# Two-layer mixer with split fp32 products: high weights times both activation halves in one matmul

## The chip, the cores and the metric

The kernel runs on one core of a Trainium2 chip. The metric is the device time of one execution in microseconds (us). The kernel before takes 1300.45 us (median of three runs, 1300.34 to 1304.79).

## The reference

One decoder layer on 256 tokens of 1024 features, all in float32. What matters here is the first half, the token mixer:

```
h = RMSNorm(x) * (1 + scale1) + shift1
z = h @ W_in       # 1024 x 9216: u v p xc B C and the gates gA gB gC, 1024 columns each
A  = W_A( u * (tril(W_s) v + b) )
Bp = scale * GroupLinear( trailing_mean_w(p) - p ),  w in 2,4,8,16
Cv = W_C( B * causal_dwconv3( C * xc ) )
x = x + gate1 * W_o( sig(gA)*A + sig(gB)*Bp + sig(gC)*Cv )
```

Then a router picks 4 of 32 experts for each token; their weights (32 x 12 MB in float32) are read from HBM one expert pair after the other, and a last RMSNorm follows.

## The kernel before

TensorE does the mixer's products in a one-pass format (fp32r). To keep float32 accuracy each operand is split in two parts, a rounded high part and the remainder (low part), and a product is the sum of three: high weights times high activations, high weights times low activations, low weights times high activations. The activations are kept as pairs: a tile `[P, 2, KB, T]` has in its second index the high (0) and the low part (1); `hp` is the pair of h, `apair` that of the branches' inner results, `fin["p"]` that of the gated sum. The weights are split as they are used: `split` (L503 to L509) has ScalarE (ACT) write the high part of 512 columns (L507) and VectorE (DVE) subtract it to get the low part (L508), into one of four buffers named `spl`.

The work is a list of steps. A `col_item` makes 128 output features of one of the products for all 256 tokens. It consists of two half-steps, each with one split of 4 x 128 weight columns and one call of `pair3` (L511): four times the two matmuls with the high weights (L515, L516), then four with the low weights (L518), all 128x256 and all accumulating into the same 256 columns of one PSUM bank (`abank`, six banks in turn). `u_item` is one such half-step with its own bank, `pool_item` has two output blocks of six matmuls for one split. When the last half-step of an item is through, an evacuation function reads the bank:

- `u_item`'s evac: first half a copy on ACT (L626), second half an addition on DVE (L628)
- `sig_evac` for gA, gB, gC: a sigmoid on ACT (L827)
- `pa_evac`, `c_evac`, `b_evac`, `pc_evac`: a product on DVE (L832, L883, L890, L898)
- `p_evac`, `xc_evac`: a copy on ACT (L838, L879); `pool_item`'s evac: a scaled product on DVE (L869)

`to_pair` (L435, L436) then splits a finished result for the next product, high part on ACT, low part on DVE. The steps `v` and `wo` do not use `pair3`; they issue their own matmuls of 512 or 256 columns (L556 to L560, L976).

The order on every engine is written out by the loop at L1036 (`AHEAD = 3`): before step i's matmuls are issued, the splits of the steps ahead are issued (at most four live), then step i's matmuls, then a row or so of the adaLN product (`weigh_rows`, L443 on DVE, `spread` there), then what is due, then the evacuation of step i-1. ACT and DVE work in the order of issue. The items come in this order: u, gA, pA, p and gB by turns, pool with xc, C, B, xc, C, B, gC, pC, wo.

Loads run through SyncE's queue into a ring of seven 2 MB slots (`lay`, `issue`, L176); a slot is loaded again when the work that read it has been issued and is done. The ring feeds the mixer and, behind it, the experts.

## Time and profile before

| | |
|---|---|
| median of three runs | 1300.45 us |
| the profiled execution | 1302.01 us, its span 1300.3 us |
| mean granted TensorE clock | 0.984 |
| PE busy | 1211.8 us (93%) |
| DVE busy | 439.8 us (34%) |
| ACT busy | 270.8 us (21%) |
| HBM read | 482 MB, 372 GB/s over the span |

The profile shows one execution. PE is TensorE's matmuls, PEld its weight loads, DVE VectorE, ACT ScalarE. An instruction has a start and a duration; neighbouring ones on one engine overlap by their durations, so the distance of two starts is what one more of them takes. The mixer lasts until about 336 us, the router follows, and the experts take the rest.

### The profile page before, as it was taken

To read this page: it belongs to the slowest core of one execution; us is meant where nothing else is said; L and a number is where in the kernel's file an instruction comes from. 1 tells how busy PE (TensorE), PEld (TensorE's weight loads), DVE (VectorE), ACT (ScalarE), POOL (GpSimd) and SP (SyncE) were. 2 spreads that over 40 slices of the span, in tenths; PEclk is the share of its full clock that TensorE was granted. 3 is DMA by queue.
4 is the path that set the end of the run, shared out by engine and by line. 5 is a ranking of instruction groups with operands and counts; after the bars stand their busy time and mean duration, and the time that the engine had idled before them with its cause. 6 is when DMAs were issued, how large, how long until landed. Compare 5 with 4: busy or idle time off the path is not lost. (4 is left out here: it accounts for less than half of the span.)

```text
span 1300.3 us, 22561 instructions
## 1 busy us (share of the span) xinstructions
PE 1211.8 (93%) x9653; PEld 613.4 (47%) x9654; DVE 439.8 (34%) x884; ACT 270.8 (21%) x538; POOL 11.0 (1%) x27
## 2 busy tenths in 40 slices
PE   7999999999899999898989899998989898998877
PEld 5899998999633333333323233333333232333222
DVE  3477886877441111212132221112121311111122
ACT  5564554455321000001010000001010000000001
POOL 0010000000000000000000000000000000000001
PEclk9999999999999999999999999999999999999989
DMA  9997198297799899999999999999999999999993
GB/s 343 325 387 246 51 384 302 106 394 306 247 381 382 353 430 427 426 428 426 426 426 427 427 385 426 428 426 427 426 428 427 427 427 426 427 426 428 410 379 135
DMA packets 83765, 484.73 MB, mean 373 GB/s; under 512 B 6753, under 2 KB 21161, under 8 KB 59854
## 3 DMA queue, kind: packets, MB, share of 16 engines
q1 hardware_dynamic: 82982, 481.51, 91.1%
q10 hardware_dynamic: 680, 1.71, 0.4%
q8 instruction: 81, 1.33, 0.4%
q14 instruction: 22, 0.18, 0.0%
HBM read 482.16 MB, written 1.05 MB: 372 GB/s over the span
## 5 line engine op out<-in xcount | busy, mean ns | idle before, releaser
L1336 PE MATMUL abank<-wchunk,b 128*32 (+2 forms) x4160 | 485.6, 603 | 39.1 <-DMA wchunk<-in_exp_w_down_dram 31.9
L1336 PEld LDWEIGHTS abank<-wchunk,b 128*32 128x32 f32 x4160 | 139.8, 112 | 349.4 <-issue 322.4
L1336 PE MATMUL cbank<-wchunk,b 128*32 128x512 f32 (+2 forms) x1952 | 231.6, 592 | 10.7 <-DMA wchunk<-in_exp_w_gu_dram 10.6
L1109 DVE TENSOR_SCALAR b<-bbank,a,mod 128x128 f32<-128x128 f32 x64 | 26.2, 410 | 396.1 <-PE bbank L1172 396.1
L508 DVE TENSOR_TENSOR spl<-wchunk,spl 128x512 fp32r<-128x512 f32 x196 | 132.1, 691 | 49.0 <-ACT spl L507 45.5
L1107 ACT ACTIVATE b<-bbank,mod,a 128x128 f32<-128x128 f32 x64 | 29.2, 457 | 540.1 <-PE bbank L1172 540.1
L507 ACT ACTIVATE spl<-wchunk 128x512 fp32r<-128x512 f32 x196 | 120.8, 627 | 76.3 <-PE abank L518 47.3
L515 PE MATMUL abank<-b,spl 128*128 128x256 f32 x432 | 110.3, 287 | 0.0
L1172 PEld LDWEIGHTS bbank<-spl,b 128*128 128x128 f32 x512 | 66.4, 193 | 91.2 <-issue 89.3
L516 PE MATMUL abank<-b,spl 128*128 128x256 f32 x432 | 108.3, 283 | 0.0
L1336 PEld LDWEIGHTS cbank<-wchunk,b 128*32 128x32 f32 x1952 | 52.8, 109 | 110.8 <-issue 94.0
L1172 PE MATMUL bbank<-spl,b 128*128 128x128 f32 x512 | 87.2, 300 | 1.8 <-DVE spl L1165 0.9
L515 PEld LDWEIGHTS abank<-b,spl 128*128 128x128 f32 x432 | 82.7, 191 | 3.6 <-issue 2.5
L1392 DVE TENSOR_TENSOR row<-abank,x 128x512 f32<-128x512 f32 (+1 forms) x32 | 21.9, 683 | 180.9 <-PE abank L1336 180.9
L516 PEld LDWEIGHTS abank<-b,spl 128*128 128x128 f32 x432 | 82.8, 192 | 0.2 <-issue 0.2
L1269 DVE TENSOR_TENSOR xt<-bbank,xt 128x512 f32<-128x512 f32 (+1 forms) x66 | 44.6, 675 | 109.5 <-PE bbank L1326 109.5
L518 PE MATMUL abank<-b,spl 128*128 128x256 f32 x432 | 69.7, 283 | 0.0
L1326 PE MATMUL bbank<-row,b 128*128 128x512 f32 (+1 forms) x132 | 62.7, 606 | 1.6 <-DVE row L1392 1.4
L518 PEld LDWEIGHTS abank<-b,spl 128*128 128x128 f32 x432 | 59.7, 192 | 0.0
L515 PE MATMUL cbank<-b,spl 128*128 128x256 f32 x224 | 57.2, 287 | 0.0
L516 PE MATMUL cbank<-b,spl 128*128 128x256 f32 x224 | 56.1, 283 | 0.0
L1319 ACT ACTIVATE b<-bbank 128x256 f32<-128x256 f32 x16 | 6.1, 383 | 235.7 <-PE bbank L1317 235.7
(272 smaller groups left out, 846.8 us busy)
## 6 DMA issues: line engine op xcount, KB each, us to landing
wchunk<-in_exp_w_gu_dram SPq DMA_DIRECT2D x125, 2048.0 KB, 17.3
wchunk<-in_exp_w_down_dram SPq DMA_DIRECT2D x56, 2048.0 KB, 15.9
wchunk<-in_w_in_dram SPq DMA_DIRECT2D x16, 2048.0 KB, 9.7
wchunk<-in_ada_w_dram SPq DMA_DIRECT2D x8, 2048.0 KB, 11.9
wchunk<-in_exp_w_down_dram SPq DMA_DIRECT2D x10, 1024.0 KB, 14.3
wchunk<-in_ada_w_dram SPq DMA_DIRECT2D x16, 512.0 KB, 9.6
wchunk<-in_exp_w_down_dram SPq DMA_DIRECT2D x10, 512.0 KB, 12.4
wchunk<-in_w_in_dram SPq DMA_DIRECT2D x4, 1024.0 KB, 10.7
```

The lines of the kernel that those rows point to most:

```text
L507: S.activation(hi, w, AF.Copy)
L508: V.tensor_tensor(lo, w, hi.bitcast(F32), op=OP.subtract)
L515: TE.matmul(out_, lhsT=wh, rhs=xh, start=first and i == 0, stop=False)
L516: TE.matmul(out_, lhsT=wh, rhs=xl, start=False, stop=False)
L518: TE.matmul(out_, lhsT=wl, rhs=xh, start=False, stop=last_ and i == n - 1)
L1107: S.activation(out_, in_, AF.Identity, scale=a2[:, k:k + 1], bias=sh2[:, k:k + 1])
L1109: V.tensor_scalar(out_, in_, a2[:, k:k + 1], sh2[:, k:k + 1], op0=OP.mult, op1=OP.add)
L1172: TE.matmul(ps, lhsT=xn2[:, tt, k * P:(k + 1) * P], rhs=oh[p][:, tt].rearrange("p a g -> p (a g)"), start=tt == 0, stop=tt == TT - 1)
L1269: V.tensor_tensor(xt[:, tt, s], ps, xt[:, tt, s], op=OP.add)
L1326: TE.matmul(ps, lhsT=wt[:, tt * P:(tt + 1) * P], rhs=wk["yv"][:, c:c + n], start=True, stop=True)
L1336: TE.matmul(out_[g * GRP:(g + 1) * GRP], lhsT=xl[:, g * GRP:(g + 1) * GRP], rhs=w(e), start=start, stop=stop, skip_group_check=True)
L1392: V.tensor_tensor(wk["yv"][:, c:c + m], bank[c], wk["g2b"][:, c:c + m], op=OP.mult)
```

## The change

`pair3` takes both activation halves as one moving operand: high weights times `x2` of 2 x 256 columns fill both halves of the PSUM bank with one 128x512 matmul, the low weights still use the high activations alone and add into the first half. So eight matmuls stand where twelve were. The two halves of the bank now have to be added: `total` copies the first half on ACT and adds the second on DVE; every evacuation but that of `u` calls it or its like, and the product or sigmoid that read the bank before reads the total in SBUF. The second `u` half-step adds both halves on DVE.

```
@@ -510,12 +510,20 @@
 
     def pair3(out_, ws, xs_, first, last_):
 
+
         n = len(ws)
-        for i, ((wh, wl), (xh, xl)) in enumerate(zip(ws, xs_)):
-            TE.matmul(out_, lhsT=wh, rhs=xh, start=first and i == 0, stop=False)
-            TE.matmul(out_, lhsT=wh, rhs=xl, start=False, stop=False)
-        for i, ((wh, wl), (xh, xl)) in enumerate(zip(ws, xs_)):
-            TE.matmul(out_, lhsT=wl, rhs=xh, start=False, stop=last_ and i == n - 1)
+        for i, ((wh, wl), x2) in enumerate(zip(ws, xs_)):
+            TE.matmul(out_, lhsT=wh, rhs=x2, start=first and i == 0, stop=False)
+        for i, ((wh, wl), x2) in enumerate(zip(ws, xs_)):
+            TE.matmul(out_[:, 0], lhsT=wl, rhs=x2[:, 0], start=False, stop=last_ and i == n - 1)
+
+    def sides(bank):
+        return bank.rearrange("p (a t) -> p a t", a=2)
+
+    def total(out_, ps):
+        S.activation(out_, ps[:, 0], AF.Copy)
+        V.tensor_tensor(out_, ps[:, 1], out_, op=OP.add)
+        return out_
 
     def col_item(name, m, pair, evac):
 
@@ -530,10 +538,10 @@
 
             def mm():
                 if hf == 0:
-                    cell["ps"] = abank()[:, :T]
+                    cell["ps"] = sides(abank())
                 hi, lo = cell[hf]
                 pair3(cell["ps"], [(hi[:, k], lo[:, k]) for k in range(4)],
-                      [(pair[:, 0, 4 * hf + k], pair[:, 1, 4 * hf + k]) for k in range(4)], hf == 0, hf == 1)
+                      [pair[:, :, 4 * hf + k] for k in range(4)], hf == 0, hf == 1)
             steps.append((prep, mm, (lambda: evac(m, cell["ps"])) if hf else None, name))
         for hf in range(2):
             one(hf)
@@ -616,16 +624,17 @@
             cell["w"] = split(w[:, :, m * P:(m + 1) * P], 4)
 
         def mm():
-            cell["ps"] = ps = (abank if h else cbank)()[:, :T]
+            cell["ps"] = ps = sides((abank if h else cbank)())
             hi, lo = cell["w"]
-            pair3(ps, [(hi[:, k], lo[:, k]) for k in range(4)], [(hhi[:, 4 * h + k], hlo[:, 4 * h + k]) for k in range(4)], True, True)
+            pair3(ps, [(hi[:, k], lo[:, k]) for k in range(4)], [hp[:, :, 4 * h + k] for k in range(4)], True, True)
 
         def evac():
             if h == 0:
                 us[m] = sigs()
-                S.activation(us[m], cell["ps"], AF.Copy)
+                total(us[m], cell["ps"])
                 return
-            V.tensor_tensor(us[m], cell["ps"], us[m], op=OP.add)
+            for a in range(2):
+                V.tensor_tensor(us[m], cell["ps"][:, a], us[m], op=OP.add)
             later(2, lambda: S.activation(us[m], us[m], AF.Gelu_apprx_tanh))
             if m == 4:
                 v_norm()
@@ -824,18 +833,18 @@
 
     def sig_evac(m, ps):
         sig[m] = sigs()
-        S.activation(sig[m], ps, AF.Sigmoid)
+        S.activation(sig[m], total(sig[m], ps), AF.Sigmoid)
 
     def pa_evac(m, ps):
         if "t" not in mix:
             mix["t"] = big.tile([P, KB, T], F32, name="b3")
-        V.tensor_tensor(mix["t"][:, m], ps, sig[m], op=OP.mult)
+        V.tensor_tensor(mix["t"][:, m], total(mix["t"][:, m], ps), sig[m], op=OP.mult)
 
 
     def p_evac(m, ps):
         w = WINDOWS[m // 2]
         pp = pads()
-        S.activation(pp[:, PAD:], ps, AF.Copy)
+        total(pp[:, PAD:], ps)
         s, lag = pp, 1
         while lag < w:
             n = sums()
@@ -860,13 +869,13 @@
 
         def mm(e):
             hi, lo = cell["w"]
-            cell[e] = abank()[:, :T]
+            cell[e] = sides(abank())
             pair3(cell[e], [(hi[:, k, e * P:(e + 1) * P], lo[:, k, e * P:(e + 1) * P]) for k in range(2)],
-                  [(apair[:, 0, 2 * g + k], apair[:, 1, 2 * g + k]) for k in range(2)], True, True)
+                  [apair[:, :, 2 * g + k] for k in range(2)], True, True)
 
         def evac(e):
             m = 2 * g + e
-            V.scalar_tensor_tensor(sig[m], cell[e], vec2[:, PS_ + m:PS_ + m + 1], sig[m], op0=OP.mult, op1=OP.mult)
+            V.scalar_tensor_tensor(sig[m], total(hfs(), cell[e]), vec2[:, PS_ + m:PS_ + m + 1], sig[m], op0=OP.mult, op1=OP.mult)
             V.tensor_tensor(mix["t"][:, m], mix["t"][:, m], sig[m], op=OP.add)
         for e in range(2):
             steps.append((prep if e == 0 else None, lambda e=e: mm(e), lambda e=e: evac(e), "pw"))
@@ -876,18 +885,18 @@
 
     def xc_evac(m, ps):
         cv[m] = sigs()
-        S.activation(cv[m], ps, AF.Copy)
+        total(cv[m], ps)
 
     def c_evac(m, ps):
         z = pads()
-        V.tensor_tensor(z[:, PAD:], ps, cv[m], op=OP.mult)
+        V.tensor_tensor(z[:, PAD:], total(z[:, PAD:], ps), cv[m], op=OP.mult)
         S.activation(cv[m], z[:, PAD - 2:PAD - 2 + T], AF.Copy, scale=vec2[:, CW + m:CW + m + 1])
         for i in (1, 2):
             V.scalar_tensor_tensor(cv[m], z[:, PAD - 2 + i:PAD - 2 + i + T], vec2[:, CW + 8 * i + m:CW + 8 * i + m + 1],
                                    cv[m], op0=OP.mult, op1=OP.add)
 
     def b_evac(m, ps):
-        V.tensor_tensor(cv[m], ps, cv[m], op=OP.mult)
+        V.tensor_tensor(cv[m], total(hfs(), ps), cv[m], op=OP.mult)
         to_pair(ap_["a"][:, 0, m], ap_["a"][:, 1, m], cv[m])
 
     fin = {}
@@ -895,7 +904,7 @@
     def pc_evac(m, ps):
         if "p" not in fin:
             fin["p"] = big.tile([P, 2, KB, T], F32R, name="b1")
-        V.tensor_tensor(sig[m], ps, sig[m], op=OP.mult)
+        V.tensor_tensor(sig[m], total(hfs(), ps), sig[m], op=OP.mult)
         V.tensor_tensor(sig[m], mix["t"][:, m], sig[m], op=OP.add)
         to_pair(fin["p"][:, 0, m], fin["p"][:, 1, m], sig[m])
```

On PE, one half-step of a gC item (`b1_155` is the pair of h, `spl` the split weights). Before:

```order
L515 MATMUL abank_2556<-b1_155,spl_2517 128x256
L516 MATMUL abank_2556<-b1_155,spl_2517 128x256
L515 MATMUL abank_2556<-b1_155,spl_2517 128x256
L516 MATMUL abank_2556<-b1_155,spl_2517 128x256
L515 MATMUL abank_2556<-b1_155,spl_2517 128x256
L516 MATMUL abank_2556<-b1_155,spl_2517 128x256
L515 MATMUL abank_2556<-b1_155,spl_2517 128x256
L516 MATMUL abank_2556<-b1_155,spl_2517 128x256
L518 MATMUL abank_2556<-b1_155,spl_2517 128x256 x4
```

After:

```order
L516 MATMUL abank_2561<-b1_155,spl_2530 128x512 x4
L518 MATMUL abank_2561<-b1_155,spl_2530 128x256 x4
```

Four matmuls of 512 columns stand for eight of 256; the four with the low weights are as they were.

On ACT, in the stretch in which p and gB items take turns (`L507` splits a weight, `L435` is `to_pair`; `L827` in the kernel before is gB's sigmoid and `L838` p's copy; in the changed one `L836` is the sigmoid, `L524` the copy in `total`). Before:

```order
L507 ACTIVATE spl<-wchunk 128x512 [waits DVE_49,PE_49]
L435 ACTIVATE b_579<-b_94 128x256 [waits DVE_49]
L827 ACTIVATE b_94<-abank 128x256
L507 ACTIVATE spl<-wchunk 128x512 [waits PE_49,Activation_49] x2
L838 ACTIVATE b_94<-abank 128x256
L507 ACTIVATE spl<-wchunk 128x512 [waits DVE_49,PE_49] x2
L435 ACTIVATE b_579<-b_94 128x256 [waits DVE_49]
L827 ACTIVATE b_94<-abank 128x256
```

After:

```order
L507 ACTIVATE spl<-wchunk 128x512 [waits PE_49,Activation_49]
L435 ACTIVATE b_555<-b_94 128x256 [waits DVE_49]
L524 ACTIVATE b_94<-abank 128x256
L836 ACTIVATE b_94<-b_94 128x256 [waits DVE_49]
L507 ACTIVATE spl<-wchunk 128x512 [waits PE_49,Activation_49] x2
L524 ACTIVATE b_94<-abank 128x256
L507 ACTIVATE spl<-wchunk 128x512 [waits PE_49,Activation_49] x2
L435 ACTIVATE b_555<-b_94 128x256 [waits DVE_49]
L524 ACTIVATE b_94<-abank 128x256
L836 ACTIVATE b_94<-b_94 128x256 [waits DVE_49]
```

The sigmoid, which needed PE alone, now stands behind `total`'s copy and waits for DVE, and the next weight splits are queued behind it.

On DVE, at the first `pC` items (`L508` the low part of a split, `L898`/`L907` the product with the gate, `L899`/`L908` the sum of the branches, `L436` `to_pair`). Before:

```order
L508 TENSOR_TENSOR spl<-wchunk,spl 128x512 [waits Activation_49] x4
L898 TENSOR_TENSOR b_94<-abank,b_94 128x256
L899 TENSOR_TENSOR b_94<-b_1137,b_94 128x256 [waits DVE_49]
L436 TENSOR_TENSOR b_3276<-b_94,b_3276 128x256 [waits Activation_49]
L508 TENSOR_TENSOR spl<-wchunk,spl 128x512 [waits Activation_49] x2
L898 TENSOR_TENSOR b_94<-abank,b_94 128x256
```

After:

```order
L508 TENSOR_TENSOR spl<-wchunk,spl 128x512 [waits DVE_49,Activation_49]
L525 TENSOR_TENSOR b_94<-abank,b_94 128x256 [waits Activation_49]
L907 TENSOR_TENSOR b_94<-b_94 128x256 [waits DVE_49]
L908 TENSOR_TENSOR b_94<-b_1029,b_94 128x256 [waits DVE_49]
L436 TENSOR_TENSOR b_2816<-b_94,b_2816 128x256 [waits Activation_49]
L508 TENSOR_TENSOR spl<-wchunk,spl 128x512 [waits Activation_49] x2
L525 TENSOR_TENSOR b_94<-abank,b_94 128x256 [waits Activation_49]
```

One addition (`L525`) that waits for ACT has come ahead of the product; the rest keeps its order.

## Rows read from the trace of the kernel before

**Rows 1.** The page: span, and matmul groups (busy us, mean ns of one).
```profile
span 1300.3 us, 22561 instructions
...
L515 PE MATMUL abank<-b,spl 128*128 128x256 f32 x432 | 110.3, 287 | 0.0
...
L515 PE MATMUL cbank<-b,spl 128*128 128x256 f32 x224 | 57.2, 287 | 0.0
```
**Rows 2.** Busy time by stretch: length, PE, PEld, DVE, ACT, POOL; clock, DMA share, GB/s.
```profile
121.80:134.20 12.40, 12.40 (x106) 12.40 (x105) 12.40 (x23) 5.17 (x9) 0.00 (x0) 1.00 0.55 201
134.20:157.00 22.80, 22.80 (x186) 21.50 (x185) 19.38 (x43) 13.16 (x28) 0.99 (x2) 1.00 0.02 3
157.00:181.00 24.00, 24.00 (x202) 24.00 (x201) 20.30 (x48) 14.13 (x30) 0.00 (x0) 1.00 1.00 362
181.00:200.00 19.00, 19.00 (x160) 17.43 (x159) 15.54 (x31) 9.83 (x19) 0.00 (x0) 1.00 1.04 383
200.00:240.00 40.00, 40.00 (x344) 37.72 (x343) 27.01 (x52) 19.51 (x39) 0.00 (x0) 1.00 0.67 244
240.00:266.20 26.20, 26.20 (x224) 24.29 (x223) 21.30 (x43) 12.35 (x24) 0.00 (x0) 1.00 0.42 151
266.20:288.50 22.30, 22.30 (x189) 22.30 (x188) 16.32 (x26) 12.59 (x25) 0.00 (x0) 1.00 1.05 395
288.50:310.30 21.80, 21.80 (x184) 21.80 (x183) 16.62 (x34) 10.02 (x20) 0.00 (x0) 1.00 0.67 285
346.00:356.00 10.00, 9.07 (x75) 3.16 (x68) 1.15 (x3) 0.14 (x1) 0.00 (x0) 0.95 0.17 47
380.00:400.00 20.00, 20.00 (x177) 6.63 (x170) 6.45 (x13) 3.35 (x5) 0.00 (x0) 1.00 0.73 296
400.00:600.00 200.00, 190.15 (x1544) 67.45 (x1544) 41.39 (x75) 17.99 (x35) 0.00 (x0) 0.99 0.99 415
```
**Rows 3.** Timeline of PE at the end of the mixer: start, duration, engine, line.
```profile
303.13 0.28 PE L515 MATMUL abank<-b,spl 128*128 128x256 f32 x1
...
304.57 0.28 PE L515 MATMUL abank<-b,spl 128*128 128x256 f32 x1
...
310.33 11.07 PE L976 MATMUL cbank<-spl,b 128*128 128x512 f32 x48
321.24 3.04 PE L976 MATMUL abank<-spl,b 128*128 128x256 f32 x24
```
**Rows 4.** Waits from 83 to 311 us: total, times, longest.
```profile
ACT spl L507 <- PE abank L518: 44.4, 64, 2.8
...
DVE b L436 <- ACT b L435: 7.9, 15, 1.1
...
DVE b L886 <- ACT b L884: 5.5, 8, 1.0
```
**Rows 5.** Timeline of DVE through one pC item.
```profile
302.81 1.29 DVE L508 TENSOR_TENSOR spl<-wchunk,spl 128x512 fp32r<-128x512 f32 x2
304.02 0.41 DVE L898 TENSOR_TENSOR b<-abank,b 128x256 f32<-128x256 f32 x1
304.47 0.42 DVE L899 TENSOR_TENSOR b<-b,b 128x256 f32<-128x256 f32 x1
305.38 0.42 DVE L436 TENSOR_TENSOR b<-b,b 128x256 fp32r<-128x256 f32 x1 [0.48 <-ACT b L435]
305.90 1.29 DVE L508 TENSOR_TENSOR spl<-wchunk,spl 128x512 fp32r<-128x512 f32 x2
```
**Rows 6.** Timeline of ACT in the same item.
```profile
304.93 0.42 ACT L435 ACTIVATE b<-b 128x256 fp32r<-128x256 f32 x1 [1.63 <-DVE b L899]
305.25 1.14 ACT L507 ACTIVATE spl<-wchunk 128x512 fp32r<-128x512 f32 x2
```
**Rows 7.** Two groups by their form, 100 to 345 us: busy us, mean ns.
```profile
L443 DVE SCALAR_TENSOR_TENSOR row<-wchunk,cond,row 128x512 f32<-128x512 f32 x16 | 11.9, 744 | 0.0
...
L827 ACT ACTIVATE b<-abank 128x256 f32<-128x256 f32 x15 | 5.5, 369 | 2.4 <-DVE b L436 2.4
```

More of the change, by code (lines that the diff above doesn't have):

```diff
@@ L513, in pair3, with sides, total @@
         n = len(ws)
-        for i, ((wh, wl), (xh, xl)) in enumerate(zip(ws, xs_)):
-            TE.matmul(out_, lhsT=wh, rhs=xh, start=first and i == 0, stop=False)
-            TE.matmul(out_, lhsT=wh, rhs=xl, start=False, stop=False)
-        for i, ((wh, wl), (xh, xl)) in enumerate(zip(ws, xs_)):
-            TE.matmul(out_, lhsT=wl, rhs=xh, start=False, stop=last_ and i == n - 1)
+        for i, ((wh, wl), x2) in enumerate(zip(ws, xs_)):
+            TE.matmul(out_, lhsT=wh, rhs=x2, start=first and i == 0, stop=False)
+        for i, ((wh, wl), x2) in enumerate(zip(ws, xs_)):
+            TE.matmul(out_[:, 0], lhsT=wl, rhs=x2[:, 0], start=False, stop=last_ and i == n - 1)
+    def sides(bank):
+        return bank.rearrange("p (a t) -> p a t", a=2)
+    def total(out_, ps):
+        S.activation(out_, ps[:, 0], AF.Copy)
+        V.tensor_tensor(out_, ps[:, 1], out_, op=OP.add)
+        return out_
     def col_item(name, m, pair, evac):
@@ L532, in mm @@
                 if hf == 0:
-                    cell["ps"] = abank()[:, :T]
+                    cell["ps"] = sides(abank())
                 hi, lo = cell[hf]
                 pair3(cell["ps"], [(hi[:, k], lo[:, k]) for k in range(4)],
-                      [(pair[:, 0, 4 * hf + k], pair[:, 1, 4 * hf + k]) for k in range(4)], hf == 0, hf == 1)
+                      [pair[:, :, 4 * hf + k] for k in range(4)], hf == 0, hf == 1)
             steps.append((prep, mm, (lambda: evac(m, cell["ps"])) if hf else None, name))
@@ L618, in mm @@
         def mm():
-            cell["ps"] = ps = (abank if h else cbank)()[:, :T]
+            cell["ps"] = ps = sides((abank if h else cbank)())
             hi, lo = cell["w"]
-            pair3(ps, [(hi[:, k], lo[:, k]) for k in range(4)], [(hhi[:, 4 * h + k], hlo[:, 4 * h + k]) for k in range(4)], True, True)
+            pair3(ps, [(hi[:, k], lo[:, k]) for k in range(4)], [hp[:, :, 4 * h + k] for k in range(4)], True, True)
         def evac():
@@ L625, in evac @@
                 us[m] = sigs()
-                S.activation(us[m], cell["ps"], AF.Copy)
+                total(us[m], cell["ps"])
                 return
-            V.tensor_tensor(us[m], cell["ps"], us[m], op=OP.add)
+            for a in range(2):
+                V.tensor_tensor(us[m], cell["ps"][:, a], us[m], op=OP.add)
             later(2, lambda: S.activation(us[m], us[m], AF.Gelu_apprx_tanh))
@@ L826, in sig_evac @@
         sig[m] = sigs()
-        S.activation(sig[m], ps, AF.Sigmoid)
+        S.activation(sig[m], total(sig[m], ps), AF.Sigmoid)
     def pa_evac(m, ps):
@@ L831, in pa_evac @@
             mix["t"] = big.tile([P, KB, T], F32, name="b3")
-        V.tensor_tensor(mix["t"][:, m], ps, sig[m], op=OP.mult)
+        V.tensor_tensor(mix["t"][:, m], total(mix["t"][:, m], ps), sig[m], op=OP.mult)
     def p_evac(m, ps):
@@ L837, in p_evac @@
         pp = pads()
-        S.activation(pp[:, PAD:], ps, AF.Copy)
+        total(pp[:, PAD:], ps)
         s, lag = pp, 1
@@ L862, in mm @@
             hi, lo = cell["w"]
-            cell[e] = abank()[:, :T]
+            cell[e] = sides(abank())
             pair3(cell[e], [(hi[:, k, e * P:(e + 1) * P], lo[:, k, e * P:(e + 1) * P]) for k in range(2)],
-                  [(apair[:, 0, 2 * g + k], apair[:, 1, 2 * g + k]) for k in range(2)], True, True)
+                  [apair[:, :, 2 * g + k] for k in range(2)], True, True)
         def evac(e):
             m = 2 * g + e
-            V.scalar_tensor_tensor(sig[m], cell[e], vec2[:, PS_ + m:PS_ + m + 1], sig[m], op0=OP.mult, op1=OP.mult)
+            V.scalar_tensor_tensor(sig[m], total(hfs(), cell[e]), vec2[:, PS_ + m:PS_ + m + 1], sig[m], op0=OP.mult, op1=OP.mult)
             V.tensor_tensor(mix["t"][:, m], mix["t"][:, m], sig[m], op=OP.add)
@@ L878, in xc_evac @@
         cv[m] = sigs()
-        S.activation(cv[m], ps, AF.Copy)
+        total(cv[m], ps)
     def c_evac(m, ps):
         z = pads()
-        V.tensor_tensor(z[:, PAD:], ps, cv[m], op=OP.mult)
+        V.tensor_tensor(z[:, PAD:], total(z[:, PAD:], ps), cv[m], op=OP.mult)
         S.activation(cv[m], z[:, PAD - 2:PAD - 2 + T], AF.Copy, scale=vec2[:, CW + m:CW + m + 1])
@@ L889, in b_evac @@
     def b_evac(m, ps):
-        V.tensor_tensor(cv[m], ps, cv[m], op=OP.mult)
+        V.tensor_tensor(cv[m], total(hfs(), ps), cv[m], op=OP.mult)
         to_pair(ap_["a"][:, 0, m], ap_["a"][:, 1, m], cv[m])
@@ L897, in pc_evac @@
             fin["p"] = big.tile([P, 2, KB, T], F32R, name="b1")
-        V.tensor_tensor(sig[m], ps, sig[m], op=OP.mult)
+        V.tensor_tensor(sig[m], total(hfs(), ps), sig[m], op=OP.mult)
         V.tensor_tensor(sig[m], mix["t"][:, m], sig[m], op=OP.add)
```

## The prediction

> **What bounds the kernel now.** I read the page first, then the busy time by stretch, then the timelines of PE, DVE and ACT where stretches were tight. In every mixer stretch from 121.8 to 310.3 us PE is busy from end to end, at full granted clock [rows 2], and the list of waits names nobody whom its matmuls wait for there. DVE is busy for 12.40 of 12.40 us in one stretch, 20.30 of 24.00 in another, 16.62 of 21.80 in the last; ACT has more room [rows 2]. So PE bounds the mixer, with DVE close behind, and ACT spends 44.4 us waiting for PE to give back a split buffer [rows 4]: that wait is the cover under which the evacuations lie today.
>
> Does the mixer's length reach the end? The DMA engines are nearly idle from 346 to 356 us (share 0.17), loaded to 0.73 from 380 to 400 us, and full afterwards at 0.99 [rows 2]. Up to 400 us the loads thus wait for the mixer and the first expert pair to free ring slots; behind that they bound the experts. A microsecond lost or gained in the mixer moves the first pair, and the full DMA stretch behind it, by the same microsecond: there is no slack behind 400 us in which to make it up. I count 1 for 1.
>
> **What goes: matmuls.** One half-step of twelve 256-column matmuls takes 304.57 - 303.13 = 1.44 us, 0.120 each. 48 matmuls of 512 columns in the same format, each with its own 128-column weights, take 321.24 - 310.33 = 10.91 us, 0.227 each [rows 3]. One such matmul replaces two of 256: 0.240 - 0.227 = 0.013 us saved. There are 432 + 224 = 656 such pairs [rows 1], so PE gains 8.5 us in all; a half-step costs 4 x 0.227 + 4 x 0.120 = 1.39 us, an item 2.78 instead of 2.88. The bounds: 0 if the two-part moving operand costs two passes, and about twice that at best. Sixteen of the 164 half-steps are u's, early in the mixer; I leave them in the gain.
>
> The rows show a surcharge per matmul that hardly depends on the columns. The Trainium skill, "TensorE: Matmul & The Clock Gate", section "Back-to-back issue gap", gives for an isolated warm matmul N/2.4 + 2.5 ns: 109.2 ns at 256 columns and 215.8 at 512, 2.6 ns saved per pair. By that rule the gain would be 1.7 us (an estimate from that page), and the forecast below 6.8 us later; the trace has 120 and 227 ns, and I go by it.
>
> **What comes: additions on DVE, copies on ACT, and an order between them.** Every u half-step and every item gets one DVE addition of 256 columns: 16 + 72 + 8 for the pool blocks = 96. On ACT a copy out of PSUM is new in 24 gates, 8 each of pA, C, B, pC and pool blocks: 64, at 0.37 us as the sigmoid out of PSUM has it [rows 7], 24 us. ACT has that room in every stretch [rows 2], and the copy mostly runs while DVE is still on the splits' low parts; I price it at nothing by itself. The addition is mostly followed by an instruction that reads its result, and such a pair starts 304.47 - 304.02 = 0.45 us apart [rows 5]; 96 x 0.45 = 43 us for DVE (0.41, its bare duration, as the low end).
>
> The order is worth more than the work. In the 24 gates ACT's sigmoid now waits for DVE's addition, and the next weight splits on ACT stand behind the sigmoid, and DVE's next low part behind those. The same ring of waits exists today in pC, where it can be measured: sum on DVE at 304.47, `to_pair` on ACT at 304.93 (0.46 later), the next split on ACT at 305.25 (0.32), its low part on DVE at 305.90 (0.65) [rows 5, 6]: 1.43 us from the start of one to the next low part, in which DVE does little. A gate's addition takes the place of that sum. Of the 1.43 I have counted 0.45 as the addition; 0.98 us per gate is lost to DVE, where DVE is behind. The low bound is nothing (where ACT waits for PE anyway), the high one 1.43.
>
> **How late may DVE be?** Four split buffers: a split can start when PE is through with the half-step four before, so three half-steps of 1.39 us are ahead of it; less 0.6 for the high part, 3.6 us. DVE's lag grows by stretch and PE stands still for what exceeds 3.6. Lag per stretch = (DVE busy before + 0.45 per addition + 0.98 per gate + waits that DVE has already) - (PE's time before - 0.104 per item) [rows 2]:
> - gA and the first half of pA, before 121.8: PE has spatial products beside, no lag.
> - 121.8 (4 pA, with adaLN rows on DVE): 12.4 + 1.8 - 12.0 = +2.2.
> - 134.2 (4 p, 4 gB): 19.4 + 3.6 + 3.9 - 22.0 = +4.9.
> - 157 (4 p, 4 gB): 20.3 + 3.6 + 3.9 - 23.2 = +4.6.
> - 181 (pool, 4 xc): 15.5 + 12 x 0.45 - 18.4 = +2.5.
> - 200 (4 C, 4 B, 4 xc): DVE already waits 5.5/8 us per C and 7.9/15 per `to_pair` [rows 4], so 27.0 + 5.4 + 4.9 - 38.7 = -1.4.
> - 240 (4 C, 4 B): 21.3 + 3.6 + 4.9 - 25.4 = +4.4.
> - 266.2 (8 gC): in the first four a gate's chain, 1.21 for two low parts + 1.43, is below 2.78, no lag; in the other four, with eight adaLN rows of 0.74 [rows 7], 8 x 0.605 + 8 x 0.74 + 4 x 1.43 - 11.1 = +5.4, of which one row falls into a gate's gap: +4.6.
> - 288.5 (8 pC): the cycle of an item is 305.90 - 302.81 = 3.09 us today [rows 5], above PE's 2.88 already, and hidden by the 3.6; with the addition 3.54 against 2.78: 8 x 0.76 = +6.1.
>
> Running through with the ceiling of 3.6: stalls of 3.5 in the second stretch, 4.6, 2.5, none (the lag falls to 2.2), 3.0, 4.6, 6.1: 24.3 us. The last lag is taken up in wo, whose splits have 2.7 us of PE time each. Net +24.3 - 8.5 = +15.8 us. The profiled execution took 1302.0 us (1300.3 and 1.7 around it), so 1317.8 against it; it lies 1.6 us above the median of the runs, and against the median that is 1316.3. I forecast 1316.
>
> Bank turnover costs nothing: six banks turn over in six items, some 17 us, and the evacuations are late by a few. SyncE's queue issues the same loads in the same order; slots come back later by the same lag, in stretches in which the ring is full (DMA share 0.02 from 134 us, 0.42 from 240) [rows 2].
>
> **Rivals.**
> 1. Only the sums of work count: ACT is far enough ahead that the ring of waits in the gates closes under PE's time. For it: ACT waits 44.4 us for PE [rows 4]. Against: the order puts the next split behind the sigmoid without exception, and where DVE is the late one ACT's lead is gone. With 0.41 per addition and no 0.98 the stretches give 12.4 + 1.6 - 12.0 = +2.0, then 19.4 + 3.3 - 22.0 = +0.7, 20.3 + 3.3 - 23.2 = +0.4, 15.5 + 4.9 - 18.4 = +2.0: 1.5 us above the ceiling at worst. Time 1300.4 - 8.5 + 1.5 = 1293, and at most 1300 if half of the pC term stays. This is the side on which the change gains; it decides if a gate costs DVE less than about 0.5 us.
> 2. Half of each: the ring closes in the gates, but pC's longer cycle and one more stretch show, 8.5 to 14 us of stalls: 1300 to 1306.
> 3. Worse: the new copies on ACT are not ready when DVE comes, because ACT too is late, so each late item pays a copy (0.37) as well; some 40 items in the stretches that stall, 15 us: 1331.
> 4. The 512-column matmul gains nothing with a moving operand in two parts: +8.5 on the forecast, 1325. For it speaks only that rows 3 have contiguous operands; the same 512 columns stream in any case.
>
> **How the numbers follow.** Forecast 0.62 (own range 1308 to 1325), rival 1 0.13, rival 2 0.10, rival 3 0.11, rival 4 0.04. The range reaches into rival 1 and to rival 3's figure: 1296 to 1331. A change of 0.5% (6.5 us, about what a measurement of this kernel tells from none) is below 1294 or above 1307: faster 0.08 (more than half of rival 1), slower 0.74 (nearly all of the forecast, rivals 3 and 4), same 0.18.
>
> **What the profile after would show.** PE: 512-column matmuls 0.227 us apart, and gaps or stretched half-steps in p/gB, gC and pC, whose releaser is ACT's or DVE's split; if PE is still busy to the full there, rival 1 holds. DVE: a pC cycle near 3.5 us, and after each gate's addition an idle gap near 1 us that ends with ACT's split. ACT: waits for PE's buffers shrink from 44 us to a few, waits of the sigmoid for DVE appear. DMA: the near-idle stretch after the router comes later by the mixer's delay, and the time from there to the end is unchanged. I am wrong if the router starts within 5 us of where it does now, or if a delay there is made up behind it.

## The result and the profile after

The changed kernel takes 1335.2 us (median of 4 runs, 1332.2 to 1337.0) against 1302.1 us (median of 4 runs of the kernel before): a ratio of 1.0244, 95% interval 1.0226 to 1.0262. The direction was forecast, the size was not: +33 us instead of +16, and 4 us beyond the upper end of the range. The profiled execution has a span of 1333.3 us. Its page, with the matmul group that answers to [rows 1] (busy us, mean ns, idle time before them and its releaser):

```profile
span 1333.3 us, 21409 instructions
...
PE 1219.7 (91%) x8997; PEld 578.5 (43%) x8998; DVE 475.0 (36%) x980; ACT 285.3 (21%) x602; POOL 11.0 (1%) x27
...
L516 PE MATMUL abank<-b,spl 128*128 128x512 f32 x432 | 121.7, 402 | 6.8 <-ACT spl L507 6.4
```

656 matmuls of 512 columns stand where 1312 of 256 stood, and in front of them there is now idle time, ended by ACT's weight splits. Before there was none [rows 1]. The waits from 60 to 345 us show the same (total, times, longest), to be held against [rows 4], whose window is 83 to 311 us:

```profile
ACT b L836 <- DVE b L525: 27.5, 23, 2.5
...
ACT spl L507 <- PE abank L518: 14.0, 17, 2.2
...
DVE b L525 <- ACT b L524: 9.3, 11, 3.6
...
PE abank L516 <- ACT spl L507: 6.4, 9, 1.4
...
PE abank L518 <- DVE spl L508: 4.9, 8, 1.4
...
PE cbank L516 <- DVE b L436: 2.5, 1, 2.5
...
PE bbank L723 <- DVE b L609: 1.4, 1, 1.4
```

The first row is the ring in the gates: the sigmoid (`L836`) waits for DVE's addition (`L525`) 23 times. The second row was the cover, 44.4 us (47.3 in this wider window), and has shrunk to 14.0. The last four rows are PE standing still, which it did in none of the mixer's stretches of [rows 2]. Idle time alone does not hold the whole loss: from 60 to 337 us PE is busy for 253.6 of 277.0 us, and in the kernel before it was busy for 249.4 of 250.0 us from 60 to 310 us, with matmuls that take some 6 us more. The granted clock reads 1.00 in both stretches, so a lower clock is not the cause.

Where the time went is read best from one event per stage: the start of a stage's last matmul with low weights, in both traces. How far PE is behind the kernel before (us), for the changed kernel and for three of the experiments below ("loads moved" has the adaLN row's loads two pA items earlier, "rest later" every evacuation but u's cut in two, "new form in part" is the last version):

| end of | changed | loads moved | rest later | new form in part |
|---|---|---|---|---|
| u | -0.1 | -0.6 | -0.5 | -1.0 |
| gA | +0.9 | +0.5 | +0.5 | -1.7 |
| pA | +5.5 | +2.6 | +2.7 | -1.1 |
| p0, gB0 | +10.2 | +4.6 | +2.1 | -1.7 |
| p1, gB1 | +13.6 | +8.0 | +1.4 | -2.3 |
| pool, xc0 | +17.9 | +12.3 | +2.0 | -2.3 |
| C0, B0, xc1 | +19.2 | +13.6 | +2.9 | -2.3 |
| C1, B1 | +19.8 | +14.1 | +3.0 | -2.3 |
| gC | +21.1 | +15.5 | +2.9 | -2.9 |
| pC (wo's first matmul) | +27.1 | +21.4 | +2.3 | -3.5 |
| wo | +30.2 | +24.6 | +2.3 | -3.5 |
| last matmul | +32.9 | +26.1 | +5.7 | -2.1 |

Single traces differ by 1 us or so before any stage that matters: at the end of u three versions with the same form of u stand at 0.0, -0.2 and -1.0. Of the last column, 1.0 us was there before the new form began.

### The profile page after: what moved, and what is told of

It is laid out like the page before. It is cut to its first block, busy times and chain, and to the rows that moved or that the text cites. A ratio compares the mean times of both kernels' runs of the same rounds, so it can differ in the third digit from the quotient of the medians.

```text
span 1333.3 us, 21409 instructions
## 1 busy us (share of the span) xinstructions
PE 1219.7 (91%) x8997; PEld 578.5 (43%) x8998; DVE 475.0 (36%) x980; ACT 285.3 (21%) x602; POOL 11.0 (1%) x27
## 5 line engine op out<-in xcount | busy, mean ns | idle before, releaser
L508 DVE TENSOR_TENSOR spl<-wchunk,spl 128x512 fp32r<-128x512 f32 x196 | 129.9, 689 | 36.6 <-ACT spl L507 34.4
L516 PE MATMUL abank<-b,spl 128*128 128x512 f32 x432 | 121.7, 402 | 6.8 <-ACT spl L507 6.4
L507 ACT ACTIVATE spl<-wchunk 128x512 fp32r<-128x512 f32 x196 | 115.7, 621 | 33.7 <-PE abank L518 14.0
L516 PEld LDWEIGHTS abank<-b,spl 128*128 128x128 f32 x432 | 73.5, 189 | 23.3 <-ACT spl L507 10.1
L518 PE MATMUL abank<-b,spl 128*128 128x256 f32 x432 | 69.7, 283 | 4.9 <-DVE spl L508 4.9
L518 PEld LDWEIGHTS abank<-b,spl 128*128 128x128 f32 x432 | 65.6, 188 | 17.4 <-DVE spl L508 8.7
L516 PE MATMUL cbank<-b,spl 128*128 128x512 f32 x224 | 63.3, 402 | 5.2 <-ACT spl L507 2.6
L516 PEld LDWEIGHTS cbank<-b,spl 128*128 128x128 f32 x224 | 38.1, 188 | 16.1 <-issue 4.3
L1335 PEld LDWEIGHTS bbank<-row,b 128*128 128x128 f32 x132 | 21.2, 188 | 42.4 <-issue 20.5
L518 PE MATMUL cbank<-b,spl 128*128 128x256 f32 x224 | 36.4, 283 | 3.2 <-DVE spl L508 3.2
```

Of the source, the lines that this page charges most:

```text
L507: S.activation(hi, w, AF.Copy)
L508: V.tensor_tensor(lo, w, hi.bitcast(F32), op=OP.subtract)
L516: TE.matmul(out_, lhsT=wh, rhs=x2, start=first and i == 0, stop=False)
L518: TE.matmul(out_[:, 0], lhsT=wl, rhs=x2[:, 0], start=False, stop=last_ and i == n - 1)
L1335: TE.matmul(ps, lhsT=wt[:, tt * P:(tt + 1) * P], rhs=wk["yv"][:, c:c + n], start=True, stop=True)
```

## The experiments

The theory behind all of them is the prediction's: the loss comes from the order, ACT and DVE waiting for each other inside one step while the next weight splits stand behind. The rivals are the work itself (DVE, ACT, or both, too full) and the queue of ACT.

### PE's gain alone

```diff
     def total(out_, ps):
-        S.activation(out_, ps[:, 0], AF.Copy)
-        V.tensor_tensor(out_, ps[:, 1], out_, op=OP.add)
-        return out_
+        return ps
...
-            steps.append((prep, mm, (lambda: evac(m, cell["ps"])) if hf else None, name))
+            steps.append((prep, mm, (lambda: evac(m, cell["ps"][:, 0])) if hf else None, name))
```
(The evacuations of u, p, xc and the pool blocks, changed alike, are left out here.)

> The changed kernel's 512-column matmuls, but every evacuation reads the bank's first half alone, in one instruction as in the kernel before (left out: the high weights times the low activations, which are computed and never read). Theory of the order (ACT and DVE wait for each other in turn): PE alone gains, 656 pairs x 0.010 us = 6.6 us, so 1295 to 1296 against 1302, and no waits of PE in the mixer. The prediction's own price, 0.013 a pair, would give 1293.5. If a 512-column matmul with a two-part operand gained nothing: 1302. If part of the changed kernel's loss came from the matmuls themselves (wider reads, banks held longer): above 1302.

Measured: 1295.9 us, ratio 0.9946 (0.9929 to 0.9964). A half-step takes 1.40 us instead of 1.44; PE starts wo 7.4 us earlier, of which 1.5 were there at the end of u's first half, and has no wait in the mixer. The wider matmul is worth about 6 us, 0.010 a pair, and not the 0.013 that I had.

### The evacuations alone

```diff
-            TE.matmul(out_, lhsT=wh, rhs=x2, start=first and i == 0, stop=False)
+            for a in range(2):
+                TE.matmul(out_[:, a], lhsT=wh, rhs=x2[:, a], start=first and i == 0 and a == 0, stop=False)
```


> The changed kernel's evacuations (copy on ACT, addition on DVE) with the twelve 256-column matmuls of before, the low activations' product going to the bank's second half; nothing left out. Theory of the order: from about 110 us PE mostly waits for split weights, so its slower matmuls hide: 1335 to 1339, at most 4 us over the changed kernel. If PE were still the bound through most of the mixer, its 6.6 us would come back in full: 1342.

Measured: 1331.9 us, 1.0228 (1.0202 to 1.0254), below what I expected. PE starts wo 27.5 us late, against 27.1 with the wide matmuls; the difference in time comes behind the mixer, where the experts took 2.5 us less in this trace (939.6 against 942.1). So in the changed kernel the 6 us are not merely outweighed, they are gone: PE arrives earlier and waits.

### The work without the order

Two runs add the same kind of work to the kernel before, with results that nobody reads; a third has both kinds at the places of the change.

```diff
+    def idle_add(bank):
+        V.tensor_tensor(bank[:, T:], bank[:, :T], xt[:, 0, :T], op=OP.add)
+    def idle_copy(bank):
+        S.activation(bank[:, T:], bank[:, :T], AF.Copy)
```
Additions:


> The kernel before, with an extra DVE addition of 256 columns out of PSUM behind each of the 96 evacuations, read by nobody. Theory of the order: outside pC an addition that nobody waits for costs little, 1 to 5 us in the two stretches in which DVE's sum then exceeds PE's time (23.0 of 22.0 us, 23.9 of 23.2); in pC, where the ring of waits exists already, it lengthens the cycle like the real one, 9 us: 1309 to 1317. Theory of the work alone: nearly the whole loss of the changed kernel, whose PE gain is not in this run: 1333 to 1342.

Copies (96 of them; 32 stand where the change adds none: 16 behind u's half-steps, whose first half had its copy before, and 16 behind p and xc):


> The kernel before, with an extra ACT copy of 256 columns out of PSUM behind each of the 96 evacuations, read by nobody. Theory of the order: ACT has the room everywhere but in pC, whose cycle it may lengthen by up to 0.37 us an item: 1302 to 1310. Theory of ACT (the copies themselves, or what is queued behind them, make the loss): 1320 or more.

Both (96 additions, 64 copies):


> The kernel before, with all the work that the change adds beside PE (a 256-column DVE addition behind each of the 96 evacuations, a 256-column ACT copy ahead of 64 of them, at the places of the change), but with results that nobody reads, so that no instruction waits for them. Theory of the order: the work alone costs next to nothing, 1302 to 1309. Theory that DVE and ACT are together too full for it: 1320 or more (the changed kernel's loss without its PE gain would be 1342).

Measured: 1305.8 us, 1.0024 (1.0009 to 1.0038), with additions; 1308.7, 1.0048 (1.0031 to 1.0065), with copies; 1308.0, 1.0040 (1.0026 to 1.0053), with both. The second line of the page of the run with additions, then of that with both:

```profile
PE 1217.9 (93%) x9653; PEld 613.9 (47%) x9654; DVE 467.4 (36%) x980; ACT 270.9 (21%) x538; POOL 11.1 (1%) x27
```
```profile
PE 1213.2 (93%) x9653; PEld 615.2 (47%) x9654; DVE 468.3 (36%) x980; ACT 288.8 (22%) x602; POOL 11.0 (1%) x27
```

DVE has 980 instructions and ACT 602, exactly as in the changed kernel, and the mixer is 3.2 us longer where the changed one loses 27. With additions alone PE starts wo 0.7 us late, even pC costs nothing. This also corrects my own expectation, which had pC's cycle grow by any addition: in this trace it is 3.24 us, against 3.09 before [rows 5] and 3.54 expected, since an addition that nobody waits for falls mostly into the gap in which DVE waits for ACT's split. Of the 5.9 us at wo in the run with copies, 5.1 were lost at the end of u and the first gA item, where it has copies that the change does not have: they queue behind DVE's additions on the same bank, ACT comes 4 us later to the scaling of v that PE needs next, PE stands still for 4.1 us, and then the granted clock reads 0.50, the lower level (1.2 GHz), for 3.4 us. From p to pC the theory of the work falls: the run with both loses 0.7 us there, the changed kernel 21.6. At two other places the work alone does cost something: the run with both loses 2.1 us in gA and pA and 1.9 in wo, where the changed kernel, with the loads moved, loses 3.1 each.

### The gates' ring opened

```diff
-        sig[m] = sigs()
-        S.activation(sig[m], total(sig[m], ps), AF.Sigmoid)
+        total(sig.setdefault(m, sigs()), ps)
+        later(1, lambda: S.activation(sig[m], sig[m], AF.Sigmoid))
```


> The changed kernel, with the 24 gates' sigmoid issued one step later, so that ACT takes the next weight split before it and no longer waits for DVE's addition there; the same work on every engine. Theory of the order: the ring is opened in gA, p/gB and gC, and the stalls of gA and first pA (5 us), part of those in p/gB (8 us) and gC (2 us) go: 1322 to 1328, with the pC part (9 us) left. Theory of the work alone (96 more additions than DVE has time for): unchanged, 1333 to 1337. Theory of ACT (64 copies too many in its queue): unchanged too, ACT has the same instructions.

Measured: 1323.3 us, 1.0165 (1.0133 to 1.0198): 12 us back with the same work, as forecast. Not as forecast is where: gA and pA stay (+6.6 us at the end of pA, 1.3 of it in gA, where PE had stood still for 0.83 and 1.45 us and the granted clock then read 0.50, the lower level, from 80.8 to 84.2 us). The gain comes in p/gB (4.1 us), the pool (1.4), gC (1.1) and pC (4.1), there presumably because DVE enters pC less late.

### pC alone, and pC with its second half later

The kernel before, with the new form in pC only; then the same with product and sum a step later and `to_pair` one more (cut from the second):

```diff
-        V.tensor_tensor(sig[m], total(hfs(), ps), sig[m], op=OP.mult)
+        h = total(hfs(), ps)
+        later(1, lambda: pc_rest(m, h))
...
-        to_pair(fin["p"][:, 0, m], fin["p"][:, 1, m], sig[m])
+        later(1, lambda: to_pair(fin["p"][:, 0, m], fin["p"][:, 1, m], sig[m]))
```


> The kernel before, with the new form (512-column matmuls, copy and addition) in the eight pC items alone. Theory of the order: an item's cycle on DVE and ACT grows from 3.09 to 3.54 us against 2.8 for PE; 8 x 0.74 = 5.9 us of lag, of which 3.6 at most are hidden by the four split buffers, and what is hidden is lost at the start of wo, where a table load on ACT stands behind the last items: +5 to +9 us, 1307 to 1311. Theory of the work alone: 16.6 + 8 x 0.45 = 20.2 us of DVE work in a stretch of 21.8, so no loss: 1301 to 1303.

> The kernel before with the new form in pC alone, as in the run that came out at 1311.4 us, but with the product, the sum and to_pair one step later than copy and addition. Same work. Theory of the order: the 9 us go, 1301 to 1304. If the loss came from the number of instructions in pC, or from the table load at the start of wo: 1308 to 1312.

Measured: 1311.4 us, 1.0066 (1.0040 to 1.0092), and 1306.9, 1.0021 (1.0007 to 1.0035), the second 3 us above what I expected. The first number fits what I expected, but not for my reason alone: in its trace the mixer and wo together are 4.5 us longer, and the rest came in the experts, which also in the second run's profile took 8 us longer though wo ended level there (that execution was the slowest of its ten, 1310.5 us). What pC does is therefore read at wo's end: 4.5 us lost with the order, none without. Timeline of PE at wo in the second run (start, duration):

```profile
310.18 11.07 PE L995 MATMUL cbank<-spl,b 128*128 128x512 f32 x48
```

Its 48 matmuls run through. They take 10.9 us. In the changed kernel the same 48 take 14.1 (337.38 to 351.45); PE, then ACT:

```profile
337.38 3.28 PE L985 MATMUL cbank<-spl,b 128*128 128x512 f32 x12 [0.48 <-ACT spl L507]
340.94 3.29 PE L985 MATMUL cbank<-spl,b 128*128 128x512 f32 x12 [0.28 <-ACT spl L507]
345.59 6.02 PE L985 MATMUL cbank<-spl,b 128*128 128x512 f32 x24 [1.36 <-ACT spl L507]
```
```profile
341.42 1.28 ACT L391 ACT_TABLE_LOAD   x1
...
342.83 0.37 ACT L524 ACTIVATE b<-abank 128x256 f32<-128x256 f32 x1
```

The last pC evacuation's copy (`L524`) stands behind the table load, DVE's addition behind the copy, and wo's next split behind those. PE waits for a split three times there, 2.1 of the 3.2 us that wo's first part takes longer.

### The row's loads on ACT

In the middle of pA ACT issues two small loads. Timeline of ACT there before, then in the changed kernel, and of DVE in the changed kernel:

```profile
117.87 0.85 ACTq L806 DMA_DIRECT2D row<-in_ada_b_dram  x2
```
```profile
121.19 4.45 ACTq L815 DMA_DIRECT2D row<-in_ada_b_dram  x2
125.68 0.38 ACT L524 ACTIVATE b<-abank 128x256 f32<-128x256 f32 x1 [3.93 <-issue]
```
```profile
126.10 0.43 DVE L525 TENSOR_TENSOR b<-abank,b 128x256 f32<-128x256 f32 x1 [3.62 <-ACT b L524]
```

The two took 4.45 us to issue, the first of them 4.13; before the change 0.85, the first 0.52. In the changed kernel an evacuation's copy waits behind it, and DVE for the copy. The loads were moved 50 us earlier, and in another run two pA items earlier:

```diff
+        if m == 1:
+            gate_bias(0), gate_bias(1)
```


> The changed kernel, with the two loads of the adaLN row's bias, which ACT issues, moved from the middle of pA to the second item of u's second half (50 us earlier); nothing left out. Theory of the issue: there ACT spent 4.1 us on issuing the first of them (0.5 before), with the new copies queued behind it; away from there 2 to 4 us come back, 1331 to 1333. If the 4 us belong to that place in ACT's program and not to the load, the gap stays in pA and the time at 1334 to 1336.

> The changed kernel, with the two loads of the row's bias issued two pA items earlier on the same queue (about 116 instead of 121 us). In the three kernels in which the first of them took 4 us, an 8 KB read of the program of one engine starts within 0.4 us of it; in the four in which it took 0.5 us, none does. If it is this coincidence: 0.5 us at the new place and 3 to 6 us back, 1329 to 1332. If the load is slow in that stretch, or its buffer is given back late: still about 4 us there, and 1334 to 1336.

Measured: 1329.3 us, 1.0205 (1.0183 to 1.0227), and 1328.9, 1.0195 (1.0170 to 1.0221): 6 us back, twice what I expected from the first. ACT in the second:

```profile
115.14 0.52 ACTq L815 DMA_DIRECT2D row<-in_ada_b_dram  x1
```

So neither the load nor the stretch is slow. What fits is a coincidence: in the three traces with a long issue (4.13, 4.04, 3.93 us) two 8 KB reads of an engine's program, at 121.6 and 123.5 us in the changed kernel, start 0.3 to 2.3 us after the issue began; in the others, where the first issue took 0.52 or 0.53, no read of 8 KB stands there (one of 16 KB does in one of them). That is a correlation over all these traces, with one deliberate shift that broke it; the mechanism is not shown. The cost is shown: with the loads two items earlier PE starts wo 5.6 us sooner, 2 us more than the 3.6 by which the issue was longer. Why it is more stays open; the lag was not made up before wo.

### Every evacuation cut in two

Except for u's: copy and addition stay; sigmoid, products, sums and `to_pair` come one step later, behind the next splits (gates as above, the others like pC), and the loads 50 us early:


> The changed kernel, with every evacuation cut in two: copy and addition where they were, what follows them (sigmoid, products, sums, to_pair) one step later, behind the next weight splits; and the bias loads moved as in the run beside it. The same work on every engine. Theory of the order: no ring is left within one step; the 12 us of the gates alone, 2 to 4 of the loads and most of the 9 of pC come back (there 3.1 us of DVE work an item stand against 2.8 of PE): 1309 to 1317. If the work on DVE or the hops inside one step decide, no more than the gates' and the loads' part comes back: 1319 to 1323.

Measured: 1307.3 us, 1.0037 (1.0025 to 1.0049). 28 of the 33 us are back with not one instruction less, more than I expected. Some 6 of the 28 are the loads', as above; the other 22 are the strongest evidence for the order.

### gA, u, and a slip

What remained sat at the end of pA (+2.7). Timeline of the changed kernel in gA, DVE and ACT through one cycle:

```profile
97.20 0.41 DVE L436 TENSOR_TENSOR b<-b,b 128x256 fp32r<-128x256 f32 x1
98.07 0.42 DVE L525 TENSOR_TENSOR b<-cbank,b 128x256 f32<-128x256 f32 x1 [0.45 <-ACT b L524]
...
99.50 1.29 DVE L508 TENSOR_TENSOR spl<-wchunk,spl 128x512 fp32r<-128x512 f32 x2 [0.15 <-ACT spl L507]
```
```profile
97.65 0.38 ACT L524 ACTIVATE b<-cbank 128x256 f32<-128x256 f32 x1 [0.86 <-DVE b L436]
98.53 0.42 ACT L836 ACTIVATE b<-b 128x256 f32<-128x256 f32 x1 [0.49 <-DVE b L525]
```

The cycle is 3.51 us (the splits' low parts start at 95.99 and 99.50), PE's is 3.24. ACT's copy waits for `to_pair`'s subtraction (`L436`), because the gate goes into the buffer that u's value is read from; then addition, sigmoid, splits follow one by one. The lag is paid in the first pA item, whose second half needs the last of these values:

```profile
111.71 0.50 PE L516 MATMUL cbank<-b,spl 128*128 128x512 f32 x1 [2.46 <-DVE b L436]
```

Another part is lost before the first gA item, where PE waits 1.4 us for DVE's scaling of v (`L609`) behind u's new additions; this half-step takes 4.62 us instead of 2.98. Two runs put u back into its old form and gA's evacuation a step later, on the kernel cut in two (the run "hybrid") and on the one with moved loads:


> The kernel with every evacuation cut in two (1307.3 us), with two more edits: the u half-steps in their old form (one product per matmul, no additions), and gA's copy and addition another step later, away from the to_pair that reads the same buffer. Its trace lost 1.65 us at the first gA item, where PE waits for a value of u's second half, and 2.7 us in the first pA item, behind gA's long cycle; the old form of u gives back 0.6 us of PE's gain. If these two are the places, 1302 to 1305; if the rest of the pool, C and gC stalls (about 4 us) moves up instead, 1306 to 1308. Below 1300 only if those go too.

> The changed kernel with the row's loads two items earlier (1328.9 us), and with u in its old form and gA's evacuation (copy, addition and sigmoid together) one step later. If u's additions and gA's reuse of u's buffers cost PE the 4.5 us up to the end of pA: 1324 to 1326, with PE at the end of pA level with the kernel before or ahead of it (2.6 us behind in the run beside it). If the lag only moves on, to the next stretch that is short: 1328 to 1330.

Measured: 1319.1 us, 1.0125 (1.0105 to 1.0145), and 1330.9, 1.0227 (1.0198 to 1.0257). The first contains a slip of mine: counting gB's and gC's delay as 0 did not leave them where they were, it put copy, addition and sigmoid into the same later step, the ring again. Its trace has PE level at the end of pA, and loses 3.3 us in p1/gB1, 3.6 in the pool and xc0, and 2.5 in gC. The second did not help: u's wait is gone (the half-step takes 2.95 us), but in gA addition and sigmoid still stand together, and the first pA item waits 2.43 us as before; PE is 0.8 us earlier at wo, no more. What u gave back went at a lower clock. Timeline of PE:

```profile
109.01 0.62 PE L516 MATMUL cbank<-b,spl 128*128 128x512 f32 x1 [2.43 <-DVE b L436]
...
110.28 1.91 PE L516 MATMUL cbank<-b,spl 128*128 128x512 f32 x4
```

Behind the wait the granted clock reads 0.50, its lower level (1.2 GHz), from 109.2 to 112.6 us; the four matmuls of 1.91 us take 1.09 at 1.00, and the two half-steps 1.5 us more than with the loads moved alone, where the same wait was followed by no fall. So neither opening the ring with the copy's wait left in (the run before, +2.6 at the end of pA) nor taking that wait out with the ring left in frees the first pA item. With the slip undone, both at once ("hybrid2"):


> The run hybrid again (evacuations cut in two, u in its old form, gA's copy and addition a step later), but with gB's and gC's sigmoid one step behind copy and addition; in hybrid a step's count fell so that both came in the same step. Theory of the order: the 9 us that PE lost in hybrid behind gA go, and so do the 4.4 us that the first of these kernels lost in gA and pA: PE reaches wo 1 to 3 us before the kernel before does, 1299 to 1304. If hybrid was slow for another reason (old form of u, gA's later evacuation): 1316 to 1321 again.

Measured: 1305.7 us, 1.0025 (1.0010 to 1.0040). The first pA item's wait shrinks to 0.9 us, and PE is level at the end of pA. The 12 us that hybrid had lost at the start of wo are gone, PE starts wo 0.3 us early; the median still is 3 us above before.

### A pure delay

```diff
-                other(after_pc)
+                other(lambda: (keep_clock(140, bbank), after_pc()))
```


> The kernel before, with 140 idle 128-column matmuls between pC and wo, as a pure delay of PE of some 30 us (0.21 us each in the first microseconds); the exact delay is read from its trace. If the experts behind pass a delay on one for one: as much later at the end as the first expert matmul is, within 2 us. If they make part of it good, less; if a late start costs more there, as the changed kernel's trace suggests (30.3 us at the experts' start, 32.9 at the end): 2 to 3 us more.

Measured: 1335.6 us, 1.0262 (1.0234 to 1.0291). Timeline of PE:

```profile
309.85 31.43 PE L102 MATMUL bbank<-ones,ident 128*128 128x128 f32 x280
341.03 11.17 PE L976 MATMUL cbank<-spl,b 128*128 128x512 f32 x48
```

wo starts 30.7 us late (341.03 against 310.33), the last matmul is 33.1 us late. So the 2.7 us that the changed kernel lost in the experts need nothing of the change. But they do not follow from a delay alone either: hybrid2 lost 3 there without one. The experts' part (from the hundredth matmul behind wo to the last) took 939.4 us in the profile of before and up to 947.6 in others; what sets it stays open.

### A version that gains

Copy and addition stay only in gA, pA, p, gB, gC and pC, each cut in two (gA's a step later and the loads early, as in the run before). u, the pool blocks, xc, C and B keep the old form.


> The run hybrid2 with the pool blocks, xc, C and B in their old form too (one product per matmul, one evacuation, no addition); the new form stays in gA, pA, p, gB, gC and pC: 384 pairs, 3.8 us of PE's time at 0.010 a pair. If the stalls left in hybrid2 were those stages' own: PE starts wo 2.5 to 4 us before the kernel before does, and the time is 1298 to 1302, at most 0.3% below it. If they only move on into gC and pC: PE level at wo, 1302 to 1306.

Measured: 1300.3 us over 12 runs, ratio 0.9980 (0.9968 to 0.9992): 0.2% below the kernel before, little but outside the interval. PE starts wo 3.5 us early, 2.4 of it gained in the stages with the new form, and waits for no split in the mixer. DVE through a pC item:

```profile
297.50 0.42 DVE L525 TENSOR_TENSOR b<-cbank,b 128x256 f32<-128x256 f32 x1
297.95 0.69 DVE L508 TENSOR_TENSOR spl<-wchunk,spl 128x512 fp32r<-128x512 f32 x1
298.56 0.42 DVE L940 TENSOR_TENSOR b<-b 128x256 f32<-128x256 f32 x1
299.02 0.42 DVE L941 TENSOR_TENSOR b<-b,b 128x256 f32<-128x256 f32 x1
299.36 0.69 DVE L508 TENSOR_TENSOR spl<-wchunk,spl 128x512 fp32r<-128x512 f32 x1
299.97 0.42 DVE L436 TENSOR_TENSOR b<-b,b 128x256 fp32r<-128x256 f32 x1
300.31 0.42 DVE L525 TENSOR_TENSOR b<-abank,b 128x256 f32<-128x256 f32 x1
```

The same six instructions (product `L940` and sum `L941` now behind the next split) take 2.81 us (297.50 to 300.31), PE's own time for an item. Here is the item in the changed kernel, then PE's matmuls that wait for it:

```profile
323.16 1.29 DVE L508 TENSOR_TENSOR spl<-wchunk,spl 128x512 fp32r<-128x512 f32 x2
324.37 0.42 DVE L525 TENSOR_TENSOR b<-cbank,b 128x256 f32<-128x256 f32 x1
324.82 0.42 DVE L907 TENSOR_TENSOR b<-b 128x256 f32<-128x256 f32 x1
325.28 0.42 DVE L908 TENSOR_TENSOR b<-b,b 128x256 f32<-128x256 f32 x1
326.19 0.42 DVE L436 TENSOR_TENSOR b<-b,b 128x256 fp32r<-128x256 f32 x1 [0.48 <-ACT b L435]
326.71 0.69 DVE L508 TENSOR_TENSOR spl<-wchunk,spl 128x512 fp32r<-128x512 f32 x1
```
```profile
323.18 1.19 PE L516 MATMUL abank<-b,spl 128*128 128x512 f32 x4 [0.48 <-ACT spl L507]
...
326.73 0.73 PE L516 MATMUL abank<-b,spl 128*128 128x512 f32 x2 [0.48 <-ACT spl L507]
```

3.55 us (323.16 to 326.71): from the addition to `to_pair` each instruction needs the result of the one before, and two gaps wait for ACT.

## Why the prediction was right in direction and wrong in size

Step by step, from the table's first two columns and the runs:

- **PE bounds the mixer, and the gain of the wide matmul.** Right in kind; 8.5 us was 6.6 (656 x 0.010): 1.9 too much. By the formula for an isolated matmul in the Trainium skill, "TensorE: Matmul & The Clock Gate", section "Back-to-back issue gap", it would have been 1.6 (656 x 2.5 ns, an estimate from that page; the prediction has 1.7). The runs, with 10 ns a pair, lie nearer to [rows 3].
- **The ring in the gates and in pC.** Shown: 12 us by opening it in the gates alone, 22 by opening it everywhere but in u (28 with the loads moved). pC's cycle, forecast at 3.54, is 3.55 us. The stalls from p0 to wo's start were forecast at 24.3 us; with the loads moved they are 18.8 (21.4 - 2.6) plus the 4.6 us that PE gains there (464 pairs), 23.5. By stretch the forecast missed by up to 2.6: pool and xc0 4.8 instead of 2.5, C to xc1 2.2 instead of none, gC 2.0 instead of 4.6. That the sum fits so well is partly luck.
- **What I charged for in that ring.** I built it as work (0.45 an addition) plus 0.98 a gate. The runs without order show that from p to pC the work costs next to nothing as long as nothing waits for it: 0.7 us for all of it, where the changed kernel loses 21.6. There nearly the whole price was in the dependence.
- **"gA and the first half of pA: no lag" failed.** With the loads moved, PE is 2.6 us behind at the end of pA, after 48 half-steps that gain 0.04 each: 4.5 us of stalls, 1.7 before the first gA item and 2.8 in the first pA item. I had looked at PE's spare time there (spatial products) and not at the chain: u's additions come ahead of v's scaling on DVE, and the gate's copy waits for `to_pair` on the same buffer, with the ring behind it. Part of this needs no order: the work alone cost 2.1 us here.
- **"The last lag is taken up in wo" failed.** wo took 27.6 us instead of 24.5 (27.64 to 24.49 from first to last matmul): 3.1. I compared splits with PE's time per step and left out that pC's last evacuations and a table load are ahead of those splits on ACT. With pC's evacuations cut in two and the table load in its place wo takes 24.5 again; the work alone cost 1.9 us here.
- **ACT's copies at nothing: failed by one wait.** The copies as work cost little (both less additions alone: 2 us). But they put the evacuations behind whatever ACT issues, and that was the load of 4 us: 5.6 us at wo's start (27.1 less 21.4 with the loads moved).
- **1 for 1 to the end.** Up to the first experts exactly; at the end +2.7, which a pure delay shows as well.

The sum: 15.8 + 1.9 (gain) - 0.8 (stalls p0 to wo's start) + 4.5 (gA, pA) + 3.1 (wo) + 5.6 (loads) + 2.7 (experts) = 32.8, and the trace has 32.9 at the last matmul. The terms come from single traces, so the small ones are good to about 1 us.

Of the rivals the first (only the sums of work), the second (half of each) and the fourth (no gain of the wide matmul) are excluded by the runs. The third, ACT late too, came nearest in time (1331), but its mechanism, a copy per late item, is not what happened: one wait of 3.6 us and two places without cover were. The range was too narrow because it held bounds for the terms that I had priced, and none for those that I had set to zero.

## What to carry to other kernels

Before adding work to an idle engine, ask what waits for its result and what stands behind the waiter on its queue; the same 160 instructions made this kernel 33 us slower in one order and 5 in another. An evacuation that needs a second engine is cut in two, with the next step's loads or splits between the halves. And a cushion of buffers is spent once: check at its end, and in front of every in-order queue that issues transfers or table loads, what is left of it.

## What the hardware showed unexpectedly

- Two neighbouring 256-column additions or products on DVE start 0.45 us apart where the second reads the first's result (324.37 to 324.82 in the changed kernel's item), and 0.34 where it does not (299.97 to 300.31 in the last version). Reordering alone makes six instructions 0.74 us shorter, the gaps included.
- The first issue of the two 2 KB loads on ACT's queue took 0.52 or 0.53 us in most traces and about 4 in three.
- The time of the kernel before mostly goes with its mean granted clock: 1299.2 to 1300.6 us at 0.985, 1302.0 to 1305.4 at 0.978 to 0.981 (five and eight of the 17 runs of one set); of the three at 0.984 two took 1299.6 and one 1303.5. A change of 3 us needs many runs on both sides.
- Four of the traces hold, between 30 us and the end of wo, a stretch of 3.4 us in which the granted clock reads 0.50, each behind waits of PE of 0.68 to 4.1 us; the changed kernel waited up to 2.46 us at a time without one. Where it could be compared, such a stretch cost 1.1 to 1.5 us, so a wait and the slower matmuls behind it are to be read separately.
